# State space mixer: two x tiles projected as one seven-product pair in the first phase, parked in DRAM and read back

## The chip, the cores and the metric

The kernel runs on one core of a Trainium2 chip. The metric is the device time of one execution in microseconds (us); a kernel's time is the median of several executions.

## The reference

One layer of a hybrid sequence model over 1024 tokens with 1024 features, batch 1, all in float32. What matters here, cut down:

```python
u = rms_norm(h, norm_w)
proj = u @ w_in                                   # 1024 x 6668 outputs, then split:
q, f_logit, i_in, g_hg, u_pool, g_pool, xbc, dt_raw, z = jnp.split(proj, ...)
o_hg   = group_rms_norm(hgrn2_mixer(q, f_logit, i_in, lb), ...) * silu(g_hg)   # 6 heads
o_pool = pool_mixer(u_pool, ...) * silu(g_pool)                                # 4 groups
xbc    = silu(causal_conv4(xbc) + conv_b)         # 1792 channels = 14 tiles of 128
xs, bm, cm = split(xbc)                           # 6 x tiles, 4 B tiles, 4 C tiles
y_ssd  = ssd(xs, bm, cm, dt) * silu(z)            # state space mixer, 4 groups of 192 channels
h = h + concat(o_hg, o_pool, group_rms_norm(y_ssd, ...)) @ w_out
h = h + sigmoid(h @ w_pg) * (p @ w_pe)
return rms_norm(h, final_norm_w)
```

The change concerns x tiles 0 and 3 of `xbc`: how and when their 2 x 128 columns of `u @ w_in` are computed. State space group 0 needs x tiles 0 and 1, group 1 tiles 1 and 2, group 2 tiles 3 and 4, group 3 tiles 4 and 5.

## The kernel before

Every float32 product is made of three matmuls: each operand is split into a high part `hi` (ScalarE, line 168) and a remainder `lo` (VectorE, line 169), and `mm3` (lines 192 to 196) adds hi*hi, hi*lo and lo*hi in PSUM. The normalized and transposed input is kept split in SBUF as `uh`, `ul`.

Weights pass through a ring: SyncE (SP) loads a 512 KB piece into `raw` (two buffers, line 161), then it is split into `hi` and `lo` (four buffers each). So a piece can be split only when the piece four before it has been multiplied for the last time, and its load is issued when a `raw` buffer comes free.

A single channel tile is projected by `cm_proj` (lines 198 to 209): for each of two halves of the tokens 8 x 3 matmuls of 128x512 into one of two `pj` banks, then an evacuation. A pair of channel tiles can be projected by `st_cm` (lines 356 to 388) instead: seven products (Strassen's scheme in Winograd's form) of 4 x 3 matmuls, in the order 1, 5, 6, 2, 7, 3, 4, with seven evacuations (four copies on ScalarE, three additions on VectorE). The sums of `u` that it needs (`SH`, `SL`) lie in SBUF until `sst.close()`; the sums of weights are made in DRAM by GpSimd's DMA queue (`sums_by_dma`, lines 125 to 132): per pair eight copies and accumulating copies, of which six form a chain t3 = b22, t3 += b12, t2 = t3, t2 += b11, t4 = t2, t4 += b21. `st_cm_w(i)` (lines 346 to 354) loads and splits a pair's four weight pieces: w0 (products 1 and 2), w1 = t1, t3 (5 and 7), w2 = t2, t4 (6 and 4), w3 (3).

The phases: normalization and the V projections; four pairs for the pooling mixer by `st_cm` (lines 494 to 532, outputs in slots of an arena `bg`); two times three-way Z and G tiles by `st_tm` (lines 390 to 436); six heads of the gated recurrence (`hg_proj`, `hg_mix`, lines 563 to 728); then the state space phase (lines 733 to 860); gates, output projection and the end.

In the state space phase `plan` gives the order of tiles per group: B, C, then x. `conv_tile` (lines 733 to 751) projects a tile with `cm_proj`, evacuates each half twice on ScalarE (line 739 copies it to `xp`, line 740 writes scale * x + bias to `y`), adds the three shifted taps on VectorE (line 748) and applies Silu (line 749). `xp` and `y` are slots of a second arena, `ar`, which gives out the slot that has been free longest. `tok_x` transposes x tiles into `Y`. `ssd_group` (lines 763 to 822) runs eight chunks, and `y_fin` (lines 827 to 839) gates and normalizes, with gate tiles that take `ar` slots too.

A scheduler orders each engine's instructions by program order as priority, moved up for splits and evacuations, and by a simulated readiness; engines then run their queues in that order. So the projections of the next group's tiles fill TensorE between the small matmuls of `ssd_group`.

Of the kernel before, what the change touches and what calls it, by code (L numbers as in the profile page):

```python
# [9 lines left out]
F32 = mybir.dt.float32  # L10
# [7 lines left out]
P = 128  # L18
S = 1024
# [58 lines left out]
def body(ctx: ExitStack, tc: tile.TileContext, x, pT, wcm, wtm, wdt, wo, wg, we, nw, fw, cst, prm, out):  # L78
# [37 lines left out]

    PAIRS_C = ((26, 27), (30, 31), (28, 29), (32, 33))
    PAIRS_T = ((5, 6), (7, 2))
    tcd = [dp.tile([P, 2048], F32, name=f"tcd{i}") for i in range(4)]
    ttd = [dp.tile([P, 4096], F32, name=f"ttd{i}") for i in range(2)]  # L120
# [15 lines left out]
    def some_sums(ins, n):  # L136

        with tc.issue_after(ins.ins):
            for _ in range(n):
                if later:  # L140
                    later.pop(0)()
# [153 lines left out]
    xst.close()  # L295
    for d, (j0, j1) in zip(tcd, PAIRS_C):
        later += sums_by_dma([d[:, i * 512 : i * 512 + 512] for i in range(4)], wcm[j0][:, :512], wcm[j1][:, :512], wcm[j0][:, 512:], wcm[j1][:, 512:])
    for d, (s0, s1) in zip(ttd, PAIRS_T):
        later += sums_by_dma([d[:, i * 1024 : i * 1024 + 1024] for i in range(4)], wtm[2 * s0], wtm[2 * s1], wtm[2 * s0 + 1], wtm[2 * s1 + 1])
    some_sums(rooted, len(later))  # L300
    later += sums_by_dma([tod[i] for i in range(4)], *(wo[i, j] for i in range(2) for j in range(2)))
# [231 lines left out]


    gzd = dp.tile([P, NT, 1024], F32, name="gzd")
    for i in range(2):
# [184 lines left out]
    for h in range(HEADS):  # L721
        hg_proj(h)
        if h + 1 < HEADS:
            cm_want(2 * h + 2)
        else:
            cm_want(12)
        hg_mix(h)
# [5 lines left out]
    def conv_tile(j, nxt):  # L733
# [8 lines left out]
        cw = lambda i: pr[:, P_CW + 4 * j + i : P_CW + 4 * j + i + 1]  # L742
        cm_proj(12 + j, ev)
        if nxt is not None:
            cm_want(nxt)
        for i in range(3):
# [95 lines left out]
    plan = ((0, (6, 10, 0, 1)), (1, (7, 11, 2)), (2, (8, 12, 3, 4)), (3, (9, 13, 5)))  # L842
    order = [12 + j for _, js in plan for j in js]
    for g, js in plan:
        held = {}
        for j in js:
            i = order.index(12 + j)
            y, yh = conv_tile(j, order[i + 1] if i + 1 < len(order) else None)
            if j < 6:
                tok_x(j, y)  # L850
                ar.give(yh)
            else:
                held[j] = (y, yh)
# [372 lines left out]
```

## Time and profile before

| | |
|---|---|
| median of 3 runs | 1039.11 us (1036.5 to 1044.67) |
| profiled execution, its own time | 1037.42 us |
| its span in the trace | 1035.5 us |
| TensorE / weight loads / VectorE / ScalarE / GpSimd busy | 95% / 81% / 64% / 48% / 12% of the span |
| mean granted TensorE clock | 0.987 of full speed |

The working of the prediction is made against the profiled execution, 1037.42 us, because its durations come from there; 1.92 us of that lie outside the span. A busy share of TensorE counts overlapping matmuls once; the time that one matmul takes from the engine is read from the distance between the starts of successive ones. "Idle before" names the time an engine waited and the instruction that ended the wait.

### The profile page before, as it was taken

What the parts mean: (1) busy time and instruction counts of PE and PEld (TensorE: products, weight loads), DVE (VectorE), ACT (ScalarE), POOL (GpSimd) and SP (SyncE); (2) the same over time, 40 slices, a digit from 0 to 9 for tenths busy, and PEclk for the clock granted to TensorE, in tenths of its full rate; (3) what the DMA queues carried; (4) which work ended last, traced back from release to release, by engine and by line L of the source; (5) the groups of instructions that cost most, each with busy time, mean ns of one, the idle gap of its engine ahead of it and who ended that gap; (6) DMA issues with size and microseconds to landing.
All of it is one profiled execution on the core that took longest, in us unless ns stands there. A gap on an engine that the chain in (4) does not pass through costs nothing.

```text
span 1035.5 us, 17385 instructions
## 1 busy us (share of the span) xinstructions
PE 987.9 (95%) x6972; PEld 835.1 (81%) x6972; DVE 664.1 (64%) x1081; ACT 496.6 (48%) x924; POOL 128.1 (12%) x202
## 2 busy tenths in 40 slices
PE   8899999999999999998999999999969999999994
PEld 7899687999877877787878787799958888888883
DVE  5692547443286678667478885878246966565776
ACT  6442343544623332333557575778424333436765
POOL 2332210000001101110101010003323000000023
PEclk9989999999999999999999999999989999999997
DMA  7799982555715277451524543234499333224535
GB/s 297 191 193 244 245 214 89 180 165 153 236 42 178 65 167 203 130 168 37 121 87 117 142 123 95 81 92 165 157 338 418 104 113 100 83 82 165 165 117 204
DMA packets 62161, 162.28 MB, mean 157 GB/s; under 512 B 6368, under 2 KB 29248, under 8 KB 60352
## 3 DMA queue, kind: packets, MB, share of 16 engines
q1 hardware_dynamic: 45040, 91.88, 27.3%
q0 software_dynamic: 14592, 65.02, 23.7%
q10 hardware_dynamic: 2448, 4.26, 1.1%
q8 instruction: 55, 0.90, 0.4%
q14 instruction: 26, 0.21, 0.1%
HBM read 136.97 MB, written 66.11 MB: 196 GB/s over the span
## 4 chain that ended last, share of the span: by engine, by line
PE 74%; DVE 11%; DMA 4%; ACT 4%; issue 1%; POOL 1%; ACTq 0%; POOLq 0%; DVEq 0%; SPq 0%
PE b_pj L194 13%; PE b_pj L195 13%; PE b_pj L196 13%; PE b_mx L196 6%; PE b_mx L194 6%; PE b_mx L195 6%; DVE ar L582 5%; PE b_sc L194 2%; PE b_sc L195 2%; PE b_sc L196 2%; DVE lo L169 1%; ACT hi L168 1%; PE b_mx L806 1%; PE b_mx L871 1%; PE b_sc L704 1%
## 5 line engine op out<-in xcount | busy, mean ns | idle before, releaser
L169 DVE TENSOR_TENSOR lo<-raw,hi 128x1024 fp32r<-128x1024 f32 (+1 forms) x114 | 137.0, 1203 | 124.4 <-ACT hi L168 117.7
L168 ACT CAST hi<-raw 128x1024 fp32r<-128x1024 f32 (+1 forms) x114 | 117.7, 1035 | 132.9 <-PE b_pj L195 53.5
L194 PE MATMUL b_pj<-uh,hi 128*128 128x512 f32 x416 | 166.6, 400 | 2.1 <-ACT ar L740 1.7
L195 PE MATMUL b_pj<-ul,hi 128*128 128x512 f32 x416 | 167.7, 403 | 0.0
L196 PE MATMUL b_pj<-uh,lo 128*128 128x512 f32 x416 | 167.2, 402 | 0.0
L194 PE MATMUL b_pj<-hi,uh 128*128 128x256 f32 (+1 forms) x320 | 93.5, 292 | 4.9 <-ACT vs L258 4.6
L582 DVE TENSOR_TENSOR ar<-ar 128x512 f32<-128x512 f32 (+8 forms) x168 | 93.9, 594 | 6.4 <-PE b_sc L673 4.9
L194 PEld LDWEIGHTS b_pj<-uh,hi 128*128 128x128 f32 x416 | 78.3, 188 | 18.8 <-ACT ar L740 3.1
L195 PE MATMUL b_pj<-lo,uh 128*128 128x256 f32 (+1 forms) x320 | 92.1, 288 | 0.0
L196 PE MATMUL b_pj<-hi,ul 128*128 128x256 f32 (+1 forms) x320 | 91.8, 287 | 0.2 <-DVE ul L247 0.2
L195 PEld LDWEIGHTS b_pj<-ul,hi 128*128 128x128 f32 x416 | 78.3, 188 | 16.9
L196 PEld LDWEIGHTS b_pj<-uh,lo 128*128 128x128 f32 x416 | 78.2, 188 | 15.8
L194 PE MATMUL b_mx<-hi,ah 128*128 128x512 f32 x192 | 76.6, 399 | 5.1 <-ACT ah L983 5.1
L983 ACT CAST ah<-q 128x1024 fp32r<-128x1024 f32 x36 | 37.5, 1048 | 84.9 <-PE b_mx L195 47.0
L196 PE MATMUL b_mx<-hi,al 128*128 128x512 f32 x192 | 75.9, 395 | 0.4 <-DVE al L984 0.4
L195 PE MATMUL b_mx<-lo,ah 128*128 128x512 f32 x192 | 76.2, 397 | 0.0
L984 DVE TENSOR_TENSOR al<-q,ah 128x1024 fp32r<-128x1024 f32 x36 | 43.7, 1222 | 47.2 <-ACT ah L983 47.2
L194 PEld LDWEIGHTS b_pj<-hi,uh 128*128 128x128 f32 x320 | 61.6, 193 | 5.6 <-ACT vs L258 4.8
L195 PEld LDWEIGHTS b_pj<-lo,uh 128*128 128x128 f32 x320 | 61.5, 192 | 0.7 <-DVE lo L169 0.5
L196 PEld LDWEIGHTS b_pj<-hi,ul 128*128 128x128 f32 x320 | 61.4, 192 | 0.5 <-DVE ul L247 0.4
L748 DVE SCALAR_TENSOR_TENSOR ar<-ar,pr 128x1021 f32<-128x1021 f32 (+2 forms) x42 | 53.7, 1279 | 2.8 <-ACT ar L740 2.3
L194 PEld LDWEIGHTS b_mx<-hi,ah 128*128 128x128 f32 x192 | 36.4, 190 | 13.9 <-ACT ah L983 5.5
(296 smaller groups left out, 2130.8 us busy)
## 6 DMA issues: line engine op xcount, KB each, us to landing
raw<-wcm SPq DMA_DIRECT2D x30, 512.0 KB, 4.4
tod<-wo POOLq DMA_DIRECT2D x4, 2048.0 KB, 15.2
raw<-tod SPq DMA_DIRECT2D x16, 512.0 KB, 3.3
raw<-wtm SPq DMA_DIRECT2D x14, 512.0 KB, 4.2
tcd<-wcm POOLq DMA_DIRECT2D x24, 256.0 KB, 8.0
ttd<-wtm POOLq DMA_DIRECT2D x12, 512.0 KB, 8.6
E<-cumd SPq DMA_DIRECT2D x32, 192.0 KB, 3.1
mt<-ar POOLq DMA_DIRECT2D x24, 256.0 KB, 2.5
```

Source lines behind the costliest of these rows:

```text
L168: A.copy(hi[:, :width], raw[:, :width])
L169: V.tensor_tensor(out=lo[:, :width], in0=raw[:, :width], in1=hi[:, :width].bitcast(F32), op=ALU.subtract)
L194: T.matmul(out=o, lhsT=sh, rhs=mh, start=first, stop=False, skip_group_check=more)
L195: T.matmul(out=o, lhsT=sh, rhs=ml, start=False, stop=False, skip_group_check=more)
L196: T.matmul(out=o, lhsT=sl, rhs=mh, start=False, stop=last, skip_group_check=more)
L582: mul = lambda o, x, y: V.tensor_tensor(out=o, in0=x, in1=y, op=ALU.mult)
L704: T.matmul(out=sb[:, :P], lhsT=kt3[:, c, :], rhs=O[:, c, hv], start=True, stop=True)
L748: V.scalar_tensor_tensor(out=y[:, d:], in0=xp[:, : S - d], scalar=cw(i), in1=y[:, d:], op0=ALU.mult, op1=ALU.add)
L806: T.matmul(out=b2[r, i * 64 : i * 64 + 64], lhsT=E[:, i, r], rhs=xd[:, c % 4, i * 64 : i * 64 + 64], start=True, stop=True)
L871: T.transpose(out=b[:, i * P : (i + 1) * P], in_=src[:, half * 4 + i, k * P : (k + 1) * P], identity=ident)
L983: A.copy(hi, src)
L984: V.tensor_tensor(out=lo, in0=src, in1=hi.bitcast(F32), op=ALU.subtract)
```

## The change

A fifth pair, wcm tiles 12 and 15 (x tiles 0 and 3), is added to the pairs. Its weight sums are issued on GpSimd's queue behind those of the `ttd` pairs. After the pooling loop and ahead of `st_tm` it is projected with `st_cm` into two slots of `bg`, and each slot is stored to a DRAM tile `park`. In the state space phase `conv_tile` loads `xp` for these tiles from DRAM on SP's queue and writes `y` with one ScalarE instruction over 1024 tokens, where it projected them and evacuated the halves. The prefetch of weights follows: the two tiles leave the list `order`, and behind the last head the first piece asked for is that of tile 18 (B of group 0), where it was tile 12.

```diff
--- before.py
+++ after.py
@@ -114,9 +114,11 @@
     ones = cs[:, C_ONE : C_ONE + P]
 
 
-    PAIRS_C = ((26, 27), (30, 31), (28, 29), (32, 33))
+    PAIRS_C = ((26, 27), (30, 31), (28, 29), (32, 33), (12, 15))
+    PARKED = [j for p in PAIRS_C[4:] for j in p]
+    parkd = {j: dp.tile([P, S], F32, name=f"park{j}") for j in PARKED}
     PAIRS_T = ((5, 6), (7, 2))
-    tcd = [dp.tile([P, 2048], F32, name=f"tcd{i}") for i in range(4)]
+    tcd = [dp.tile([P, 2048], F32, name=f"tcd{i}") for i in range(5)]
     ttd = [dp.tile([P, 4096], F32, name=f"ttd{i}") for i in range(2)]
 
     tod = dp.tile([4, 4 * P, 1024], F32, name="tod")
@@ -293,10 +295,12 @@
     nc.sync.dma_start(cs, cst[:, P:])
     nc.sync.dma_start(pr, prm)
     xst.close()
-    for d, (j0, j1) in zip(tcd, PAIRS_C):
+    for d, (j0, j1) in zip(tcd[:4], PAIRS_C):
         later += sums_by_dma([d[:, i * 512 : i * 512 + 512] for i in range(4)], wcm[j0][:, :512], wcm[j1][:, :512], wcm[j0][:, 512:], wcm[j1][:, 512:])
     for d, (s0, s1) in zip(ttd, PAIRS_T):
         later += sums_by_dma([d[:, i * 1024 : i * 1024 + 1024] for i in range(4)], wtm[2 * s0], wtm[2 * s1], wtm[2 * s0 + 1], wtm[2 * s1 + 1])
+    for d, (j0, j1) in zip(tcd[4:], PAIRS_C[4:]):
+        later += sums_by_dma([d[:, i * 512 : i * 512 + 512] for i in range(4)], wcm[j0][:, :512], wcm[j1][:, :512], wcm[j0][:, 512:], wcm[j1][:, 512:])
     some_sums(rooted, len(later))
     later += sums_by_dma([tod[i] for i in range(4)], *(wo[i, j] for i in range(2) for j in range(2)))
     later += sums_by_dma([tgd[i] for i in range(4)], *(wg[i, j] for i in range(2) for j in range(2)))
@@ -530,6 +534,14 @@
             bg.give(Uh)
         bg.give(G0h)
         bg.give(G1h)
+
+
+    W = st_cm_w(4)
+    outs = [bg.take(1024) for _ in range(2)]
+    st_cm(W, outs[0][0], outs[1][0])
+    for j, (z, zh) in zip(PAIRS_C[4], outs):
+        nc.sync.dma_start(parkd[j], z)
+        bg.give(zh)
 
 
     gzd = dp.tile([P, NT, 1024], F32, name="gzd")
@@ -723,7 +735,7 @@
         if h + 1 < HEADS:
             cm_want(2 * h + 2)
         else:
-            cm_want(12)
+            cm_want(12 + 6)
         hg_mix(h)
 
 
@@ -740,9 +752,13 @@
             A.activation(y[:, c], b, AF.Identity, scale=cw(3), bias=pr[:, P_CB + j : P_CB + j + 1])
 
         cw = lambda i: pr[:, P_CW + 4 * j + i : P_CW + 4 * j + i + 1]
-        cm_proj(12 + j, ev)
-        if nxt is not None:
-            cm_want(nxt)
+        if 12 + j in PARKED:
+            nc.sync.dma_start(xp, parkd[12 + j])
+            A.activation(y, xp, AF.Identity, scale=cw(3), bias=pr[:, P_CB + j : P_CB + j + 1])
+        else:
+            cm_proj(12 + j, ev)
+            if nxt is not None:
+                cm_want(nxt)
         for i in range(3):
             d = 3 - i
             V.scalar_tensor_tensor(out=y[:, d:], in0=xp[:, : S - d], scalar=cw(i), in1=y[:, d:], op0=ALU.mult, op1=ALU.add)
@@ -840,11 +856,11 @@
 
 
     plan = ((0, (6, 10, 0, 1)), (1, (7, 11, 2)), (2, (8, 12, 3, 4)), (3, (9, 13, 5)))
-    order = [12 + j for _, js in plan for j in js]
+    order = [12 + j for _, js in plan for j in js if 12 + j not in PARKED]
     for g, js in plan:
         held = {}
         for j in js:
-            i = order.index(12 + j)
+            i = order.index(12 + j) if 12 + j in order else len(order)
             y, yh = conv_tile(j, order[i + 1] if i + 1 < len(order) else None)
             if j < 6:
                 tok_x(j, y)
```

## Rows read from the trace of the kernel before

**Rows 1.** The page, part 1: busy time, share of span, instructions

```profile
PE 987.9 (95%) x6972; PEld 835.1 (81%) x6972; DVE 664.1 (64%) x1081; ACT 496.6 (48%) x924; POOL 128.1 (12%) x202
```

**Rows 2.** The page, part 4: chain that ended last, by engine

```profile
PE 74%; DVE 11%; DMA 4%; ACT 4%; issue 1%; POOL 1%; ACTq 0%; POOLq 0%; DVEq 0%; SPq 0%
```

**Rows 3.** Busy time per stretch: stretch, length, engines, clock, DMA share, GB/s

```profile
95.00:185.00 90.00, 87.36 (x364) 66.39 (x363) 51.61 (x83) 34.65 (x51) 11.19 (x16) 1.00 0.74 195
130.00:160.00 30.00, 30.00 (x131) 24.21 (x130) 14.62 (x16) 11.65 (x15) 2.80 (x5) 1.00 0.86 221
160.00:185.00 25.00, 23.79 (x97) 17.43 (x96) 17.28 (x26) 10.68 (x15) 0.00 (x0) 1.00 0.25 83
...
496.20:528.40 32.20, 32.20 (x151) 26.59 (x152) 16.17 (x16) 15.78 (x30) 4.70 (x4) 1.00 0.52 124
528.40:577.00 48.60, 46.99 (x302) 38.25 (x301) 39.21 (x73) 32.23 (x73) 4.62 (x6) 1.00 0.44 125
577.00:637.30 60.30, 59.54 (x365) 48.67 (x364) 44.17 (x78) 38.63 (x83) 4.62 (x6) 1.00 0.40 114
637.30:687.00 49.70, 48.61 (x336) 40.20 (x335) 40.86 (x78) 35.59 (x77) 2.58 (x4) 1.00 0.30 88
```

**Rows 4.** TensorE's instructions in order of time (start, duration): a pair's product; the Z and G tiles' first

```profile
95.12 0.40 PE L194 MATMUL b_pj<-sh,hi 128*128 128x512 f32 x1
...
97.91 0.39 PE L194 MATMUL b_sc<-uh,hi 128*128 128x512 f32 x1
...
184.70 0.28 PE L194 MATMUL b_mx<-hi,uh 128*128 128x256 f32 x1
```

**Rows 5.** The same, one half of x tile 0's projection: 24 matmuls

```profile
501.77 0.39 PE L194 MATMUL b_pj<-uh,hi 128*128 128x512 f32 x1
...
507.21 0.40 PE L194 MATMUL b_pj<-uh,hi 128*128 128x512 f32 x1
```

**Rows 6.** ScalarE in order of time, the hand-over behind the fourth pair

```profile
177.78 1.05 ACT L168 CAST hi<-raw 128x1024 fp32r<-128x1024 f32 x1 [2.05 <-PE b_sc L195]
```

**Rows 7.** GpSimd's queue in order of time, the tail of the weight sums

```profile
113.19 0.84 POOL L129 DMA_DIRECT2D tcd<-wcm  x1 [1.26 <-DMA tcd<-tcd]
...
129.29 0.81 POOL L129 DMA_DIRECT2D ttd<-wtm  x1 [5.77 <-DMA ttd<-ttd]
...
152.64 0.81 POOL L129 DMA_DIRECT2D ttd<-wtm  x1 [6.88 <-DMA ttd<-ttd]
```

**Rows 8.** DMA issues: count, KB each, median us to landing

```profile
raw<-wcm SPq DMA_DIRECT2D x30, 512.0 KB, 4.4
...
tcd<-wcm POOLq DMA_DIRECT2D x24, 256.0 KB, 8.0
...
raw<-tcd SPq DMA_DIRECT2D x8, 512.0 KB, 6.9
```

**Rows 9.** Groups of ScalarE's instructions, 496 to 710 us: busy, mean ns, idle before

```profile
L740 ACT ACTIVATE ar<-b_pj,pr 128x512 f32<-128x512 f32 x26 | 20.2, 779 | 0.0
...
L749 ACT ACTIVATE ar<-ar 128x1024 f32<-128x1024 f32 x13 | 13.8, 1059 | 16.5 <-DVE ar L748 16.5
L168 ACT CAST hi<-raw 128x1024 fp32r<-128x1024 f32 x13 | 13.6, 1044 | 11.9 <-PE b_pj L195 11.9
```

**Rows 10.** VectorE in order of time, between state space groups 1 and 2

```profile
605.86 0.95 DVE L833 TENSOR_TENSOR ar<-ar 128x768 f32<-128x768 f32 x1
...
607.92 1.22 DVE L169 TENSOR_TENSOR lo<-raw,hi 128x1024 fp32r<-128x1024 f32 x1
609.06 3.92 DVE L748 SCALAR_TENSOR_TENSOR ar<-ar,pr 128x1021 f32<-128x1021 f32 x3
...
617.62 3.92 DVE L748 SCALAR_TENSOR_TENSOR ar<-ar,pr 128x1021 f32<-128x1021 f32 x3
```

**Rows 11.** VectorE in order of time, within the last head's mixing

```profile
471.77 0.35 DVE L884 SCALAR_TENSOR_TENSOR big<-big,rsh,ar 128x128 f32<-128x128 f32 x1 [1.86 <-DMA ar<-gzd]
```

**Rows 12.** Waits of TensorE, 458 to 493 us: total, times, longest

```profile
PE b_sc L595 <- DVE ar L582: 3.2, 2, 2.7
```

## The prediction, written before the change was run

> **What bounds the kernel now.** I read the page's shares of busy time first [rows 1]: TensorE is busy for 95% of the span and its weight loads for 81%, VectorE for 64%. The chain that ended last says the same in its own way: 74% of it lies on TensorE, 11% on VectorE [rows 2]. A busy TensorE is not yet a bound, so I went to the stretches that the change touches [rows 3]. From 95 to 185 us, where the pairs of the pooling mixer run, TensorE is busy for 87.4 of 90 us; in the four stretches of the state space phase it stands still for 0.0, 1.6, 0.8 and 1.1 us. In both places a matmul taken away or added is therefore time, to first order. The second reading of the same rows is VectorE: 51.6 of 90 us in the first phase, but 39.2 of 48.6, 44.2 of 60.3 and 40.9 of 49.7 us around groups 1 to 3. There it is the engine that is next to bind once TensorE has less to do.
>
> **The matmuls.** The distance between the starts of two products of a pair is 97.91 - 95.12 = 2.79 us for twelve matmuls, 0.2325 us each [rows 4]. A half of x tile 0's projection takes 507.21 - 501.77 = 5.44 us for 24 matmuls, 0.2267 us each [rows 5]. The change removes two tiles of 2 x 24, which is 96 matmuls or 21.8 us, from the state space phase, and adds seven products of twelve, which is 84 matmuls or 19.5 us, to the first phase. The balance is -2.3 us: this is all that the arithmetic can give, 0.2% of the time. Whatever waits arise at either end are of the same size, so the rest of the working is about those.
>
> **First phase, the new pair itself.** It starts where the Z and G tiles start now, at 184.70 us [rows 4]. Its four pieces are split as the fourth pair lets go of its own. In the present hand-over to the Z tiles the same thing is seen: the first split of the next weights starts at 177.78 us, released by a product of the pair still running [rows 6], seven us ahead of the first use. So the hand-over costs nothing as long as the pieces are there; without that cover it would be a load and a split, 4.4 + 1.0 + 1.2 us [rows 8, 9, 10]. The added splits and evacuations (3.5 pieces on both engines, four evacuations on ScalarE and three on VectorE, each at most as long as a split; so at most 8 us on either by [rows 9, 10]) lie in a phase where VectorE is idle for 38 of 90 us and ScalarE for 55 [rows 3]. They cost nothing. The two stores to DRAM wait on SP for the last evacuation; the loads of the next weights run ahead of them in the ring, as the pooling outputs' stores do now. I put them at nothing, and at one load, 4.4 us [rows 8], if they stand ahead of a weight load.
>
> **The weight sums.** Eight more DMAs on GpSimd's queue, six of them in a chain, are behind the `ttd` pairs. The queue waits for each link: its last issue now is at 152.64 us, one pair's last addition comes 16 us (113.19 to 129.29) or 23 us (129.29 to 152.64) behind the previous one's [rows 7]. By that distance the new pair's last addition is issued at 169 to 176 us and lands some 8 us later [rows 8], at 177 to 184. It is needed by product 6, two products into the pair, at 184.7 + 5.6 = 190.3 us, less a split of 1 to 2 us and a load of 4.4 to 6.9 [rows 8]: the sums have to have landed by 181 to 184. This just fits. From below: behind 152.64 nothing else uses the queue and the DMA share falls from 0.86 to 0.25 [rows 3], so links would be faster and the cost is nothing. From above: if the whole chain began only at 152.64, six links of 8 us end at 200 us, 17 us late. Pairs are interleaved on this queue, or their last additions could not lie 16 and 23 us apart where six links of 8 us make 48; so I take the lower end, zero.
>
> [...]
>
> The other price of the sums is that they share the DMA engines with weight loads. `raw<-tcd` loads, which run beside the sums, take 6.9 us where the weight loads as a whole take 4.4 [rows 8]. I add 1 us for the fourth pair's later loads, between 0 and 2.5 us (that difference).
>
> **State space phase, x tile 0.** Around group 0 VectorE is busy for 16.2 of 32.2 us [rows 3]. With 10.9 us of matmuls gone it has 14.9 us of work left in 21.3 (one split of 1.22 less [rows 10]), ScalarE about 13.6. The chain that follows the last projected tile (evacuation, taps, Silu, transposes) is still covered by the next group's matmuls. Its load waits for a slot that head 5 frees at its end, and the taps fall where VectorE had gaps. I put it at 0.5 us, between 0 and 2.
>
> **State space phase, x tile 3.** This one is tighter. The stretch from 577.0 to 637.3 us would become 49.4 us with 42.9 us of VectorE work. Its neighbours, with three projected tiles each, are the best row for what such a stretch needs: VectorE is idle there for 48.6 - 39.2 = 9.4 and 49.7 - 40.9 = 8.8 us [rows 3]. If this stretch needs 9.1 as well, it lasts 52.0 us, and 2.6 us of the gain go back. The mechanism that I expect is a slot. The `xp` of tile 3 lies where `y_fin` of group 1 has its gate tiles, whose last use starts at 605.86 us [rows 10]; then load (4.4), ScalarE (1.1) and the taps (3.9) bring tile 3 to about 616. `y` of tile 4 gets the slot of tile 3's `xp`, so its evacuation (L740) can't be written before that, though its first half is projected by about 611. ScalarE and then a `pj` bank wait behind it. From below 0, if VectorE fills its gaps; from above 8 us, when the tile's whole taps, load and write-out become exposed (3.9 + 4.4). I take 2.6.
>
> ScalarE itself is relieved: at least four L740 evacuations and two splits (5.2 us) against two passes of 1.06 us [rows 9].
>
> **The changed prefetch.** Tile 18 is asked for before the last head's mixing, not behind it. Its matmuls run within that mixing today, so its weights are there in time, and I count nothing. VectorE waits there 1.86 us for a DMA of a gate that was moved up [rows 11], and TensorE once 2.7 us for VectorE [rows 12]; that wait may move or go, 0 to -2.7.
>
> **Sum.** 1037.4 - 21.8 + 19.5 + 1 (loads beside the sums) + 0.5 (tile 0) + 2.6 (tile 3) = 1039.2 us. This is against the profiled execution; the median of the runs shown is 1.7 us above it, so 1039 is also the median of before. A measurement of this kernel can tell about 1% (10 us) from no change.
>
> **Rivals.**
> *The sums are late* (slower). Place: SP's load of t2, t4, behind which stand w3 and the Z pieces. It decides from a landing at 184 us; each us after that is a us. Against it: the fill of earlier gaps. For it: the distance of 23 us, by which it lands at 184, and the extra traffic. Time 1039 + 5 = 1044, at the far end 1039 + 17 = 1056.
> *VectorE and the slots take tile 3's gain* (slower). If tile 4's evacuation stands in ScalarE's queue ahead of what VectorE needs, the 8 us are exposed: 1039.2 - 2.6 + 8 = 1045; with 2 us at tile 0, 1047. For it: 87% of VectorE in that stretch. Against it: the stretches at 81 and 82% run with TensorE idle for 1.6 and 1.1 us.
> *All of the gain is kept* (faster). VectorE's idle 16 us around group 2 shrink with the stretch, no wait arises, and the 2.7 us wait in the last head goes: 1037.4 - 2.3 - 2.7 = 1032.4.
>
> **Chances.** Forecast (1035 to 1043) 0.58; late sums 0.16; VectorE and slots 0.14; all kept 0.12. The range reaches to the faster rival and over the near part of both slower ones, 1032 to 1049. Slower by over 1% of 1039.1 (above 1049.5) needs the far half of the late sums, or both slower rivals together: 0.11. Faster by over 1% (below 1028.7) would need more waits to go than the rows show: 0.04. Within 1%: 0.85.
>
> **What would show it.** The tiles of the new pair: 84 matmuls in 19.5 us, no idle time of TensorE before its third product (else the sums are late, with SP's wait on `tcd` beside it). The last `tcd` addition on GpSimd's queue at 169 to 176 us. The stretch around group 0 at 21 to 22 us and around group 2 at 50 to 53. Idle time of TensorE ended by L740 in the latter would be the slot. It would be wrong if the phases between, the heads or the end, change their own length: nothing that I found moves work into them but two memsets of `big` that shift behind the Z tiles, into idle time of VectorE.

## The result, and the profile after

The changed kernel takes 1051.0 us (1049.1 to 1053.7) against 1039.2 for the kernel before beside it: a ratio of 1.0107, 95% interval 1.0083 to 1.0131. It is 1.1% slower, outside the range of 1032 to 1049. The profiled execution of after has 1050.76 us of its own and a span of 1048.9; that of before has 1037.42 and 1035.5.

The page of after, part 1 and the first line of part 4 (compare [rows 1, 2]):

```profile
PE 991.7 (95%) x6960; PEld 836.0 (80%) x6960; DVE 667.5 (64%) x1086; ACT 494.9 (47%) x922; POOL 131.7 (13%) x210
PE 68%; DVE 13%; DMA 6%; ACT 5%; issue 1%; POOL 1%; POOLq 0%; ACTq 0%; DVEq 0%; SPq 0%
```

The shares of busy time hardly move, and there are twelve matmuls fewer, yet TensorE is busy for 3.8 us more. In the chain TensorE's part falls from 74% to 68% and that of DMAs rises from 4% to 6%. VectorE's part rises from 11% to 13%. The page says that waits came in, not where. For that I laid landmarks of TensorE's timeline side by side: the distance from the start of one landmark to the next, in one profiled execution of each kernel.

```
stretch (us)                            before    after   forecast  after - before
start to the small matmuls (bcum)       102.26    97.91   as before      -4.35
bcum to the end of the fourth pair       82.44    92.15   +1             +9.71
the new pair                               -      19.45   19.5          +19.45
Z products, to head 0's first scores    107.37   107.96   as before      +0.59
heads 0, 1, 2 (three stretches)         103.90   104.13   as before      +0.23
heads 3 and 4                            69.32    72.38   as before      +3.06
head 5 to group 0, group 0 to 1         112.90   102.31   -10.4         -10.59
group 1 to 2, group 2 to 3              109.04   105.77   -8.3           -3.27
group 3 to the fills, and the rest      348.27   346.84   as before      -1.43
```

The matmuls came out as worked: the new pair takes 19.45 us, and what x tile 0 gives is within 0.2 us. Four lines are off by several microseconds: the start, the four old pairs, heads 3 and 4, and x tile 3. The start's -4.35 us is idle time of TensorE: 9.3 us before, 4.9 after; its longest wait there, for a ScalarE evacuation of the V projections, lasts 4.6 us before and 2.2 after. None of the added instructions runs in that stretch, and over the runs below its length moves by as much.

**The old pairs.** Waits of TensorE in after between 97 and 191 us (total, times, longest); in order of time three splits of ScalarE and one of VectorE with what they waited for; last, before's split that stands for the one at 139.30:

```profile
PE b_mx L196 <- ACT big L373: 5.2, 4, 3.0
PE b_sc L522 <- DVE big L516: 3.7, 1, 3.7
...
139.30 1.05 ACT L170 CAST hi<-raw 128x1024 fp32r<-128x1024 f32 x1 [7.36 <-DMA raw<-tcd]
158.51 1.05 ACT L170 CAST hi<-raw 128x1024 fp32r<-128x1024 f32 x1 [3.84 <-DMA raw<-tcd]
164.28 0.62 ACT L170 CAST hi<-raw 128x512 fp32r<-128x512 f32 x1 [4.72 <-DMA raw<-wcm]
164.93 0.69 DVE L171 TENSOR_TENSOR lo<-raw,hi 128x512 fp32r<-128x512 f32 x1 [4.05 <-ACT hi L170]
...
140.18 1.05 ACT L168 CAST hi<-raw 128x1024 fp32r<-128x1024 f32 x1 [4.13 <-DMA raw<-tcd]
```

While ScalarE waits 7.36 us for the sums of a later pair, the evacuation of a finished product (L373) stands behind that split in its order of time, at 142.62 us, and TensorE waits for that product's bank, 3.02 us up to 145.20. The load that it waits for takes 8.8 us from issue to landing, 5.6 in before, where the split waits 4.13 us and TensorE does not wait behind it. The wait of 3.7 us goes through VectorE's queue: the split at 164.93 stands still for 4.05 us, and behind it stand the pooling additions (165.54 to 172.84 us) whose result L522 multiplies. In before TensorE waits 2.6 us in this stretch, in after 9.1. Most of the rest of the 9.71 us is the clock (stretch, length, busy time of the five engines, granted clock, DMA share, GB/s):

```profile
97.90:190.06 92.16, 83.20 (x330) 62.02 (x331) 44.99 (x63) 32.40 (x46) 15.85 (x23) 0.96 0.79 197
144.00:152.00 8.00, 6.80 (x29) 5.56 (x30) 2.64 (x5) 3.29 (x5) 1.09 (x2) 1.00 1.02 335
172.00:180.00 8.00, 7.10 (x13) 3.61 (x13) 3.64 (x8) 1.87 (x3) 0.00 (x0) 0.61 0.14 25
172.90:180.00 7.10, 7.10 (x13) 3.61 (x13) 2.74 (x6) 1.87 (x3) 0.00 (x0) 0.63 0.03 6
190.06:209.52 19.46, 19.46 (x86) 15.75 (x85) 9.15 (x10) 7.25 (x10) 0.00 (x0) 1.00 0.50 170
```

Behind the idle time of 3.71 us (it ends at 172.90) the granted clock is 0.63 for 7.1 us, 0.50 up to 178.0 and 0.95 in the last 2 us; if TensorE's time goes with the clock, that is 7.1 x 0.37 = 2.6 us, an estimate. At 0.50 one matmul of 512 columns follows another after 0.42 us there (176.91 and 177.33), against 0.23 us at 1.00 [rows 4]. Behind the 3.02 us at 145.20 it stays at 1.00. The last row is the new pair: no idle time in it at all.

**x tile 3.** After, in order of time, the engines around group 2:

```profile
623.41 0.95 DVE L849 TENSOR_TENSOR ar<-ar 128x768 f32<-128x768 f32 x1
624.38 0.32 SPq L756 DMA_DIRECT2D ar<-park  x1
631.85 1.23 ACT L757 ACTIVATE ar<-ar,pr 128x1024 f32<-128x1024 f32 x1
633.11 1.28 DVE L764 SCALAR_TENSOR_TENSOR ar<-ar,pr 128x1021 f32<-128x1021 f32 x1 [0.76 <-ACT ar L757]
635.60 0.96 DVE L855 TENSOR_TENSOR ar<-ar,rsy 128x768 f32<-128x768 f32 x1 [1.21 <-POOL rsy L158]
636.48 2.60 DVE L764 SCALAR_TENSOR_TENSOR ar<-ar,pr 128x1022 f32<-128x1022 f32 x2
639.17 1.45 ACT L752 ACTIVATE ar<-b_pj,pr 128x512 f32<-128x512 f32 x2 [2.90 <-DVE ar L764]
640.00 0.80 PE L196 MATMUL b_pj<-uh,hi 128*128 128x512 f32 x1 [4.38 <-ACT ar L752]
```

This is the chain of the prediction, link for link: the gate's multiplication frees the slot (623.41), the parked tile's load is issued, ScalarE's pass, the taps, then tile 4's evacuation (L752), which has stood still for 2.90 us, and TensorE, which has stood still for 4.38. Only the length differs: from the gate to the end of the taps it takes 639.08 - 623.41 = 15.7 us where the prediction had 10. ScalarE first evacuates a half of tile 12, loads a table (1.28 us) and applies Silu to tile 8 (the pass starts 7.5 us behind the load's issue, not 4.4), and `y_fin`'s last product (L855), itself waiting for GpSimd, stands between the first and the second tap. The clock then does the rest, on the same columns:

```profile
640.00:645.00 5.00, 5.00 (x15) 4.12 (x16) 4.96 (x8) 1.89 (x3) 0.00 (x0) 0.50 0.84 211
645.00:652.20 7.20, 7.13 (x41) 5.85 (x40) 1.41 (x3) 4.07 (x8) 0.00 (x0) 0.94 0.37 109
```

Five microseconds at 0.50 and 7.2 at 0.94 cost 2.5 + 0.4 = 2.9 us, by the same estimate; from 640.59 to 643.15 us one matmul of 512 columns follows another after 0.43 us. With the 4.38 that is 7.3, of the 10.9 - 3.3 = 7.6 us that tile 3 lost.

**Heads 3 and 4.** Both have a wait of TensorE that before does not have. After, TensorE in order of time, and the stretch between the two:

```profile
435.30 0.21 PE L607 MATMUL b_sc<-ar 128*32 128x16 f32 x2 [1.22 <-issue]
471.60 0.26 PE L607 MATMUL b_sc<-ar 128*32 128x16 f32 x8 [1.55 <-issue]
...
435.30:471.60 36.30, 33.65 (x383) 27.28 (x382) 24.61 (x55) 12.23 (x32) 3.34 (x4) 1.00 0.59 154
```

"issue" means that the profile shows nothing that was waited for. Both stand inside a run of 64 small score products, ahead of the last 2 and the last 8. From the one to the other there are 383 matmuls and 382 weight loads. Nothing in the change touches the heads; what it does is to put 84 matmuls, with as many weight loads, ahead of them in TensorE's stream. That became a theory of its own.

The page's list of DMA queues has one more row that bears on it, `q8 instruction`; here it is for the whole of after, and for 432.9 to 433.0 and 469.3 to 469.4 us (transfers that start there, MB, share of the DMA engines):

```profile
q8 instruction: 54, 0.88, 0.3%
...
q8 instruction: 1, 0.02, 55.9%
...
q8 instruction: 1, 0.02, 58.9%
```

Each of the 54 transfers is 16,384 bytes, and there is one for every 258 of the 13,920 matmuls and weight loads: by that count I take it that TensorE's own instructions come in; the trace does not show what a transfer holds. One starts 2.4 us before the first wait ends, one 2.2 us before the second.

### The profile page after: what moved, and what is told of

Read it like the earlier page. It is cut to its first block, busy times and chain, and to the rows that moved or that the text cites. A ratio compares the mean times of both kernels' runs of the same rounds, so it can differ in the third digit from the quotient of the medians.

```text
span 1048.9 us, 17396 instructions
## 1 busy us (share of the span) xinstructions
PE 991.7 (95%) x6960; PEld 836.0 (80%) x6960; DVE 667.5 (64%) x1086; ACT 494.9 (47%) x922; POOL 131.7 (13%) x210
## 4 chain that ended last, share of the span: by engine, by line
PE 68%; DVE 13%; DMA 6%; ACT 5%; issue 1%; POOL 1%; POOLq 0%; ACTq 0%; DVEq 0%; SPq 0%
PE b_pj L196 11%; PE b_pj L197 11%; PE b_pj L198 10%; PE b_mx L196 6%; PE b_mx L198 6%; PE b_mx L197 6%; DVE ar L594 5%; PE b_sc L196 2%; PE b_sc L197 2%; PE b_sc L198 2%; DMA raw<-tcd 2%; DMA E<-cumd 2%; ACT hi L170 2%; DVE lo L171 2%; PE b_mx L822 1%
## 5 line engine op out<-in xcount | busy, mean ns | idle before, releaser
L170 ACT CAST hi<-raw 128x1024 fp32r<-128x1024 f32 (+1 forms) x116 | 119.5, 1032 | 135.7 <-PE b_pj L197 46.8
L196 PE MATMUL b_pj<-uh,hi 128*128 128x512 f32 x384 | 154.9, 404 | 6.1 <-ACT ar L752 6.1
L198 PE MATMUL b_pj<-uh,lo 128*128 128x512 f32 x384 | 155.8, 406 | 0.0
L197 PE MATMUL b_pj<-ul,hi 128*128 128x512 f32 x384 | 155.8, 406 | 0.0
L196 PEld LDWEIGHTS b_pj<-uh,hi 128*128 128x128 f32 x384 | 72.8, 190 | 21.6 <-ACT ar L752 6.9
L197 PEld LDWEIGHTS b_pj<-ul,hi 128*128 128x128 f32 x384 | 72.7, 189 | 16.0
L198 PEld LDWEIGHTS b_pj<-uh,lo 128*128 128x128 f32 x384 | 72.7, 189 | 14.7
L1000 DVE TENSOR_TENSOR al<-q,ah 128x1024 fp32r<-128x1024 f32 x36 | 43.7, 1223 | 50.2 <-ACT ah L999 50.2
```

Of the source, the lines that this page charges most:

```text
L170: A.copy(hi[:, :width], raw[:, :width])
L196: T.matmul(out=o, lhsT=sh, rhs=mh, start=first, stop=False, skip_group_check=more)
L197: T.matmul(out=o, lhsT=sh, rhs=ml, start=False, stop=False, skip_group_check=more)
L198: T.matmul(out=o, lhsT=sl, rhs=mh, start=False, stop=last, skip_group_check=more)
L1000: V.tensor_tensor(out=lo, in0=src, in1=hi.bitcast(F32), op=ALU.subtract)
```

## The experiments

Three theories, each with its rivals. *Traffic*: the eight sums take DMA time that weight loads need. *Slot*: tile 3's place in the third group makes tile 4 wait. *Position*: the heads wait for instructions at places that the 84 added matmuls have shifted. All ratios are against runs of the kernel before on the same chip.

### The sums alone, added to the kernel before

```diff
+    for d, (j0, j1) in zip(tcd[4:], ((12, 15),)):
+        later += sums_by_dma([d[:, i * 512 : i * 512 + 512] for i in range(4)], wcm[j0][:, :512], wcm[j1][:, :512], wcm[j0][:, 512:], wcm[j1][:, 512:])
```

The lines stand behind those of the `ttd` pairs; no instruction reads these sums.

> The kernel before with nothing added but the eight DMAs that make the weight sums of a fifth pair, which nobody reads. Theory A (the sums cost by standing in the way of the weight loads): the pooling pairs end 5 us later than at 184.7 us, with waits of ScalarE for raw<-tcd and raw<-wcm and of TensorE for an evacuation behind them, and the time is 1039.1 + 5.4 = 1044.5 us (1043 to 1046). Theory B (the waits that the changed kernel shows there come with its run, whose first 95 us were 4.4 us shorter, and are not caused by the sums): no change, 1039 us (1037.5 to 1040.5).

Measured: 1045.8 us, ratio 1.0053 (1.0024 to 1.0083), so 5.5 us (2.5 to 8.6). Old pairs 92.88 us, heads 3 and 4 at 34.6 and 34.7, the way from head 5 to group 0 1.7 us longer, the other groups as before. TensorE's waits between 98 and 192 us, and ScalarE's split that stands for the 7.36 us of after:

```profile
PE b_mx L194 <- ACT big L371: 5.1, 2, 3.5
PE b_sc L520 <- DVE big L514: 2.8, 1, 2.8
PE b_sc L520 <- DVE big L515: 1.4, 1, 1.4
...
142.14 1.05 ACT L168 CAST hi<-raw 128x1024 fp32r<-128x1024 f32 x1 [7.86 <-DMA raw<-tcd]
```

It follows that the sums alone bring the stall of the old pairs, without a new matmul.

### The new pair with plain weights, without the sums

```diff
-    for d, (j0, j1) in zip(tcd[4:], PAIRS_C[4:]):
-        later += sums_by_dma([d[:, i * 512 : i * 512 + 512] for i in range(4)], wcm[j0][:, :512], wcm[j1][:, :512], wcm[j0][:, 512:], wcm[j1][:, 512:])
-        w1 = wsplit(wload(tcd[i][:, :1024], 1024), 1024)
+        w1 = wsplit(wload(tcd[i][:, :1024] if i < 4 else wcm[j0], 1024), 1024)
-        w2 = wsplit(wload(tcd[i][:, 1024:], 1024), 1024)
+        w2 = wsplit(wload(tcd[i][:, 1024:] if i < 4 else wcm[j1], 1024), 1024)
```

> The changed kernel without the eight DMAs of the fifth pair's sums: its pieces w1 and w2 are loaded from the weights themselves, so x tiles 0 and 3 are not the reference's and the output is another. Everything else is as in the changed kernel. Theory A: the waits of the pooling pairs go and 5.4 us come back, 1045.6 us (1044 to 1047). Theory B: 1051 us (1049.5 to 1052.5).

Measured: 1048.7 us, ratio 1.0083 (1.0058 to 1.0108). Old pairs 82.25 us; the same split of ScalarE waits 2.97 us. Heads 3 and 4 at 35.7 and 36.2, group 0 to 1, 1 to 2 and 2 to 3 at 50.2, 54.4 and 50.8. The stretch agrees with the traffic. In the time, though, taking the sums out of the changed kernel gives 2.5 us where adding them to the kernel before cost 5.5; the intervals overlap. One reason is that the moment at which the old pairs begin varies between executions as well (97.9 to 104.5 us over these kernels, the shifted starts below aside), and a late begin meets fewer of the sums. Over all profiles, the stretch is 87.5 to 92.9 us in the six with early sums and 81.8 to 86.8 in the eight without; they begin 1.9 us earlier with the sums, by the means, and end 5.2 later. The begin counts by itself: of the eight, the three that begin at 99.1 to 100.0 us need 84.9 to 85.8, the four that begin behind 102.2 need 81.8 to 82.4 (the eighth, the removal in the new order, begins at 102.12 and needs 86.79); among the six the begin makes no such order. By the eight, some 3 us of after's 9.71 may go with its early begin, so the table's first two lines are best read together. The load behind the split takes 7.6 to 9.3 us in the six and 4.4 to 8.9 in the eight: it is not the sums alone that slow it. I put the sums at 2.5 to 5.5 us.

### A slot of its own for the parked tile

```diff
+    xpk = a2p.tile([P, 1024], F32, name="xpk")
-        (xp, xh), (y, yh) = ar.take(1024), ar.take(1024)
+        (xp, xh) = (xpk, None) if 12 + j in PARKED else ar.take(1024)
+        y, yh = ar.take(1024)
```

> The changed kernel, with a tile of its own for what is read back from DRAM, so that neither that load nor the output of tile 4 waits for a slot in turn. Slot theory: the stretch between the first TensorE product of group 1 and of group 2, now 55.9 us, falls to 49 to 51 us, the 4.4 us of idle time of TensorE and the stretch at the lower clock behind it go, and the time is 1051 - 6 = 1045 us (1043.5 to 1046.5). Rival (VectorE is short of time there, whatever the slots): the stretch stays at 54 to 56 us and the time at 1050 us (1049 to 1052).

Measured: 1049.2 us, ratio 1.0093 (1.0057 to 1.0128). Group 1 to 2, then 2 to 3: 48.5 and 50.3 us (after: 55.9 and 49.9), and the longest wait of TensorE there is 1.3 us. The slot was the cause. The time barely moves, because the way to head 0 is 5.6 us longer (113.55 us): with a free slot the parked tile's load is issued early, ahead of others on SP, ScalarE waits 7.3 us for a load of E and TensorE 3.0 us for ScalarE's evacuation. The repair made a new wait on a queue:

```profile
282.69 0.41 SPq L759 DMA_DIRECT2D xpk<-park  x1
308.05 1.28 ACT L802 ACTIVATE E<-E,sm 128x128 f32<-128x128 f32 x4 [7.27 <-DMA E<-cumd]
313.31 0.79 PE L196 MATMUL b_pj<-uh,hi 128*128 128x512 f32 x1 [3.04 <-ACT ar L586]
```

### The third group takes tile 3 first

```diff
-    plan = ((0, (6, 10, 0, 1)), (1, (7, 11, 2)), (2, (8, 12, 3, 4)), (3, (9, 13, 5)))
+    plan = ((0, (6, 10, 0, 1)), (1, (7, 11, 2)), (2, (3, 8, 12, 4)), (3, (9, 13, 5)))
```

> The changed kernel with one line different: the third group takes x tile 3 from DRAM before it projects tiles 8 and 12, instead of behind them. Slot theory: the tile's load no longer waits for the gate tiles of the group before, and no evacuation waits for its taps. Group 1 to group 2 (first products with E of each) takes 49 to 51 us instead of 55.9, the longest idle time of TensorE there stays under 1.5 us and the granted clock stays at 0.9 or more; the kernel takes about 1046 us. Rival (VectorE has too much work in that stretch, wherever the tile stands): 54 to 56 us, no gain, about 1051 us. Neither theory moves the heads or the first phase.

Measured: 1044.4 us, ratio 1.0031 (1.0007 to 1.0055): 6.6 us below the changed kernel by the medians, which come from two chips, and 7.9 by the ratios. Group 1 to 2: 52.1 us, a microsecond more than expected; groups 0 to 3 together 201.6 us against 208.1. Order of time, and the only longer wait of TensorE there:

```profile
610.72 1.24 ACT L757 ACTIVATE ar<-ar,pr 128x1024 f32<-128x1024 f32 x1 [0.28 <-PE b_sc L818]
613.96 0.95 DVE L849 TENSOR_TENSOR ar<-ar 128x768 f32<-128x768 f32 x1
...
PE b_pj L196 <- ACT ar L752: 1.6, 2, 1.2
```

The parked tile's pass now stands ahead of the gate's multiplication, not 8 us behind it. The rival, too much work for VectorE, falls. Of the 21.8 us that the removed matmuls are worth, the groups now keep 221.9 - 201.6 = 20.3.

### Position: tiny matmuls in the kernel before, and in the changed one

```diff
+    tiny = bank("sc")
+    for i in range(84):
+        T.matmul(out=tiny[:, :16], lhsT=uh[:, 0, :P], rhs=uh[:, 0, :16], start=True, stop=True)
```

These lines stand ahead of the Z products. The changed kernel gets the same with 44 in place of 84.

> The kernel before with 84 matmuls of 16 columns added ahead of the Z products (their result is not used): as many TensorE instructions as the new pair has, with next to no work, no weights, no transfers. Theory that the heads' new idle times come from the position of the instructions in TensorE's stream: the two idle times without a releaser ahead of score products appear in heads 3 and 4, 1 to 1.8 us each, and these two heads last 1.3 to 1.8 us longer than the 34.6 us of before. Rival (something that the pair leaves behind, such as its stores or a shifted order of the loads): heads 3 and 4 stay at 34.6 us. The time itself: before + 5 to 8 us for the 84 matmuls, and + 3 us by the theory.

Measured: 1056.5 us, ratio 1.0161 (1.0130 to 1.0192). Heads 3 and 4 take 36.6 and 36.0 us, and the two waits are there, ahead of the last 2 and the last 8 again:

```profile
426.68 0.21 PE L600 MATMUL b_sc<-ar 128*32 128x16 f32 x2 [1.83 <-issue]
...
462.48 0.26 PE L600 MATMUL b_sc<-ar 128*32 128x16 f32 x8 [1.02 <-issue]
```

The price of the 84 was missed: they take 12.9 us (185.30 to 198.23), and the Z products behind them 2.7 us more. The first part of that row of matmuls and the rest, on the columns of [rows 3]:

```profile
185.30:190.80 5.50, 5.50 (x51) 5.50 (x49) 4.90 (x5) 2.79 (x4) 0.00 (x0) 0.98 0.75 233
190.90:198.20 7.30, 7.30 (x36) 7.30 (x36) 0.89 (x1) 0.00 (x0) 0.00 (x0) 0.50 0.35 134
```

TensorE never stands still in it, and yet the granted clock falls to 0.50; one of these matmuls follows another after 0.11 us at first and after 0.21 then.

> The changed kernel with 44 matmuls of 16 columns added ahead of the Z products (their result is not used). If what counts in the heads is where the instructions lie in TensorE's stream, a further shift moves the idle times elsewhere in a head, and may put them where TensorE is not short of instructions: heads 3 and 4 then last 34.6 us instead of 36.0 and 36.4, at a price of 2.5 to 4 us for the 44 matmuls. Rival (the position plays no part): both heads stay at 36.0 and 36.4 us, with the waits ahead of the same products.

Measured: 1059.5 us, ratio 1.0188 (1.0173 to 1.0203). Heads 3 and 4 take 34.62 and 34.75 us, no such wait is left anywhere in the heads; the stretch from head 3 to head 5 falls from 72.4 to 69.4 us. The 44 cost 6.6 us, again more than expected, and the Z products behind them take 1.4 us more. So 84 added matmuls bring the waits and 128 take them away, whatever the matmuls compute: the position theory stands.

From the first wait to the second there are 382 matmuls and 382 weight loads (the row above counts one at its border), in each of the seven kernels that have the waits: 764 instructions. Before has 55 transfers of 16,384 bytes on the queue `q8 instruction` for 13,944 matmuls and weight loads, one for every 253.5, and after 54 for 13,920, one for every 257.8; over all kernels there are 54 or 55 for 13,752 to 14,112. So 764 instructions are about three transfers, and in after the one ahead of the second wait (469.36 us) is the third behind the one ahead of the first (432.93). By the same counts, an estimate, 128 added matmuls with their loads, 256 instructions, are about one transfer: they would put the transfers back to where none added leaves them.

That TensorE waits for such a transfer is inferred from when the waits end. There are 14 of them, 0.9 to 1.8 us long, and whatever its length each ends 2.2 to 2.5 us after a transfer has started (in after 2.37 and 2.24). In the seven kernels without the waits no transfer starts from 6.7 us ahead of that run of 64 products to 3.1 us behind its start, in either head (in before's head 4 the nearest start 7.8 us ahead and 3.8 us behind). The added matmuls move the transfers, and the waits come and go with them. No run slows a transfer by itself. Why this run of products shows the wait is an argument: its 64 products of 16 columns take 0.74 us together in before, less than the 2.2 us, where 24 matmuls of 512 columns take 5.44 [rows 5].

### The removal alone, in the old order and in the new

```diff
-    for d, (j0, j1) in zip(tcd[4:], PAIRS_C[4:]):
-        later += sums_by_dma([d[:, i * 512 : i * 512 + 512] for i in range(4)], wcm[j0][:, :512], wcm[j1][:, :512], wcm[j0][:, 512:], wcm[j1][:, 512:])
...
-    W = st_cm_w(4)
-    outs = [bg.take(1024) for _ in range(2)]
-    st_cm(W, outs[0][0], outs[1][0])
...
-            nc.sync.dma_start(xp, parkd[12 + j])
+            nc.sync.dma_start(xp, wcm[12 + j])
```

> The change without the new pair and without its eight weight sums: x tiles 0 and 3 are read from DRAM where another array of that size stands (their values are not the reference's), so only the removal of the 96 matmuls is left. By the working of the prediction, with tile 3's slot at the 6.5 us that the changed kernel shows: 1037.4 - 21.8 + 0 + 6.5 = about 1022 us, group 0 in 52 us, group 1 to 2 in 55 to 56 us, heads at 34.6 us each and the stretch of the pooling pairs at 82 us. Rival (the tail of the kernel gives part of it back, or the heads' waits come from reading the parked tiles): 1027 us or more, or heads 3 and 4 at 36 us.

Measured: 1028.4 us, ratio 0.9890 (0.9860 to 0.9920). Heads at 34.6 to 34.7 us, group 0 to 1 and 1 to 2 at 49.7 and 54.2, old pairs 82.2. The groups keep 221.9 - 206.5 = 15.4 of the 21.8 us and so lose 6.4, as expected. But by the medians only 12 us are gained, and the time is where the rival has it; in the profiled execution the remaining 3 us lie ahead of the pairs (104.47 us) and in the last stretch (326.7), where executions differ by as much.

> The removal of the 96 matmuls alone (x tiles 0 and 3 read from another array in DRAM, so their values are not the reference's; no pair, no sums), with x tile 3 taken first in the third group. If the slot was all that was lost of the removal, groups 0 to 3 take 201 to 203 us together (222 in the kernel before, 206 in the removal with the old order) and the kernel about 1024 us, 4 us below the removal with the old order. If VectorE's load is what keeps part of it back, they stay at 206 us and the kernel at 1028 us.

Measured: 1023.5 us, ratio 0.9842 (0.9811 to 0.9873), as expected; groups 0 to 3 together 201.6 us. So the new order is worth 4.9 us here and 6.6 in the changed kernel, and the removal at its best is worth 16 us. A pair that takes 19.45 us can't be paid from that. This profile also shows that the old pairs are near a stall even without the sums (on the columns of [rows 3], and a wait):

```profile
140.00:150.00 10.00, 6.83 (x30) 5.20 (x29) 4.28 (x4) 6.31 (x8) 0.81 (x1) 0.99 0.57 132
150.00:160.00 10.00, 10.00 (x39) 7.96 (x38) 3.30 (x5) 2.70 (x3) 1.35 (x2) 0.84 0.70 238
...
PE b_mx L196 <- ACT big L371: 3.3, 2, 3.2
```

The stretch took 86.79 us there, the longest without sums.

### The pair behind the Z products, and the causes mended together

```diff
-    W = st_cm_w(4)
...
     for i in range(2):
...
         st_tm(i, gz_fin)
+    W = st_cm_w(4)
...
+            if g == 2:
+                with tc.issue_after(G.tensor_copy(out=seen0, in_=U[:, 0:1]).ins):
+                    while fifth:
+                        fifth.pop(0)()
```

The pair moves as a whole; its sums, in `fifth`, are issued behind the third pooling tile. In the second kernel below they are issued behind the fourth (`g == 3`), and the third group has the new order as well.

> The changed kernel with the fifth pair behind the Z and G tiles, and its sums issued only when the pooling mixer's third group has its first output, past the loads that they slowed. Theory A: the pooling pairs end at 181 to 185 us without the waits on raw<-tcd, the pair costs its 19.5 us elsewhere, and 1051 - 5.4 = 1045.6 us result (1044 to 1047.5). Theory B: 1050 to 1052 us, since nothing that matters was moved.

Measured: 1049.0 us, ratio 1.0080 (1.0048 to 1.0112). Old pairs 84.9 us, the Z products at 184.84 us (184.70 in before), Z products and pair 127.3 us, where 107.37 + 19.45 = 126.8 are expected from the two apart. Heads 3 and 4 at 36.6 and 37.0, group 0 to 1 and 1 to 2 at 52.5 and 54.7, the rest at 327.0. The traffic is gone from the old pairs; heads and groups keep their loss.

> Two of the causes mended together: the new pair stands behind the Z products and its weight sums are issued behind the last pooling tile, and the third group takes x tile 3 first. If the causes are apart and add up, the first phase up to the Z products takes 82.5 to 85 us, the Z products and the new pair together 127 us, groups 0 to 3 together 202 to 204 us (222 in the kernel before), heads 3 and 4 still 36.5 and 37 us, and the kernel about 1044 us. Rival (the causes share a resource and do not add up): over 1048 us.

Measured: 1044.1 us, ratio 1.0046 (1.0028 to 1.0064), as expected in time. Old pairs 85.8, Z products and pair 129.2 (2 more than expected), heads 3 and 4 at 36.2 both, groups together 200.7 us. But the new order alone already took 1044.4: moving pair and sums adds nothing to it. The old pairs end 4.2 us earlier; 1.8 are lost in the Z products and the pair, 2.0 in the stretch behind the state space groups (326.7 against 324.7 us). In the kernels with the early pair that last stretch took 323.4 to 325.1 us, in the others 325.6 to 327.0. Why is open; TensorE's idle time behind group 3 is much the same in both (7.8 to 8.8 us).

The last two runs move the heads' instructions from the very start of the kernel instead:

```diff
-    for i in range(WARM):
-        T.matmul(out=warm[:, :256], lhsT=blk[0].rearrange("p c t -> p (c t)")[:, :P], rhs=blk[1].rearrange("p c t -> p (c t)"), start=True, stop=True)
+    for i in range(WARM + 22):
+        n = 256 if i < 4 else 32
+        T.matmul(out=warm[:, :n], lhsT=blk[0].rearrange("p c t -> p (c t)")[:, :P], rhs=blk[1].rearrange("p c t -> p (c t)")[:, :n], start=True, stop=True)
```

`WARM` is 7; this is an edit of the changed kernel. Each of these f32 matmuls leaves two matmul records in the trace (14 for the 7 of before, 58 for the 29 here), so by the records 22 more move the stream by 44 places.

> The changed kernel with the same 22 further small matmuls among the warm-up matmuls at the very start and nothing else. Position theory: heads 3 and 4 last 34.6 us instead of 36.0 and 36.4, so about 1048 us, 3 us less than the changed kernel. Rival (the added matmuls ahead of the Z products had changed something else in the heads): heads as in the changed kernel, 1051 us.

Measured: 1056.4 us, ratio 1.0165 (1.0135 to 1.0194). The heads did what the position theory says: 34.61 and 34.80 us, no such wait. The time rose nevertheless, and the start says why (the shifted kernel first, then before: the warm-up matmuls, the first transposes behind them, and a stretch on the columns of [rows 3]):

```profile
1.38 11.19 PE L154 MATMUL b_sc<-blk,blk 128*128 128x256 f32 x58 [1.38 <-POOL blk L150]
12.38 1.95 PE L241 MATMUL b_mx<-ident,x 128*128 128x128 f32 x8
...
10.00:20.00 10.00, 9.30 (x43) 8.56 (x42) 4.12 (x6) 4.76 (x8) 2.37 (x4) 0.50 0.84 345
```

```profile
1.38 5.50 PE L151 MATMUL b_sc<-blk,blk 128*128 128x256 f32 x14 [1.38 <-POOL blk L148]
8.48 1.09 PE L238 MATMUL b_mx<-ident,x 128*128 128x128 f32 x8 [1.61 <-DVE x L229]
...
10.00:20.00 10.00, 8.51 (x62) 7.33 (x62) 8.61 (x11) 7.78 (x15) 3.62 (x8) 1.00 0.97 398
```

The added matmuls don't fit into the time in which TensorE waits: the warm-up lasts until 12.57 us, and the first transposes start at 12.38 (8.48 in before, 8.12 in after). And the granted clock is 0.50 from 10 to 20 us, where before has 1.00 and after 0.83. The bcum landmark comes at 104.94 us, not at after's 97.91. My "no cost" was wrong. The edit adds narrow matmuls and narrows three wide ones; which of the two the clock follows is not shown.

The same edit in the kernel with the late pair and the new order:

> The kernel with the late pair and the new order, with 22 further small matmuls among the warm-up matmuls at the very start (three of the wide ones become narrow), where TensorE waits for its first input. This moves every later TensorE instruction by as many places as the 44 small matmuls of the other run did, at no cost. Position theory: heads 3 and 4 last 34.6 us again, 4 us less than without the shift, and the kernel takes about 1040 us, the time of before: the change can then be had for nothing, but gains nothing either. If this beats before by more than 3 us, the working of what the pair itself costs is too high; if the heads keep 36.5 and 37 us, the shift's place matters and not its size.

Measured: 1049.6 us, ratio 1.0088 (1.0053 to 1.0122). Heads 3 and 4 at 34.6 and 34.9, 2.8 us less than without the shift; the start costs 8.6 us more (107.69). Had the shift been free, 1044.1 - 2.8 would be about 1041 us: no version of this change that these runs point to is faster than the kernel before.

## Why the prediction was wrong

**Arithmetic.** Right for the matmuls. 84 matmuls in 19.45 us, no idle time in the pair; the sums' last `tcd` addition on GpSimd's queue lies at 169.48 us, within 169 to 176:

```profile
153.81 0.83 POOL L131 DMA_DIRECT2D ttd<-wtm  x1 [5.91 <-DMA ttd<-ttd]
...
169.48 0.80 POOL L131 DMA_DIRECT2D tcd<-wcm  x1 [4.05 <-DMA tcd<-tcd]
```

The rival of the late sums is out. The hand-over to the pair, the stores, and the changed prefetch cost nothing that can be seen; tile 0 lost 10.9 - 10.59 = 0.3 us, the forecast was 0.5. One comparison is off: the sum of 1039.2 is built on a profiled execution of 1037.4 and so says 1.8 us more than before, but it was set beside before's median, as no change. Like for like it is 1040.9 by the medians.

**The loads beside the sums: the term was mis-sized, 1 us forecast, 5.5 measured alone (2.5 to 8.6).** The step that failed is "I add 1 us for the fourth pair's later loads, between 0 and 2.5 us (that difference)". It priced the traffic as a longer latency of one load. But the engines were full there: the share of 0.86 stood in [rows 3] and was read as a background. From 100 to 170 us, stretch by stretch of 10 us, the DMA shares add up to 5.80 in before and 6.60 in after: 8 us more of full occupation, and 2 MB at the 221 GB/s of [rows 3] would have said 9.5. Weight loads that were due beside it came late (8.8 us for the one that ScalarE waited for, 9.3 in the kernel with the sums alone, 5.6 in before, though up to 8.9 in one kernel without sums), the queues of ScalarE and VectorE carried the delay to TensorE, and the clock added to it. The sum of the prediction should have held this as a time of a full resource.

**Tile 3: the mechanism was right, the term was mis-sized, 2.6 us forecast, 7.6 measured.** The failing step is to take 2.6 from the neighbours' idle time of VectorE, while the slot's chain, named two sentences on, gives the later date. Two of its links were too short, and a stall of 4.4 us was priced as 4.4 us: the granted clock of 0.50 and 0.94 behind it adds 2.9 by the estimate above. The bound of 8 us held. The rival on VectorE and the slots named place and chain, but priced 1045 to 1047 by itself, since it was the only slower term at work in it.

**The heads: 3.1 us forecast as nothing.** The prediction says that it would be wrong if the heads changed their own length, and they did, by a cause that no row of before shows: with the 84 added matmuls TensorE has two waits without a releaser, of 1.22 and 1.55 us, that end 2.4 and 2.2 us after a transfer on the instruction queue starts. That it waits there for its own instructions is inferred from these times and from the counts. The shift by 84 matmuls is enough to bring it and a further 44 to remove it.

**Sum.** 11.6 us lie between the sum of 1039.2 and the profiled execution of after, 1050.76. Start and old pairs together 9.7 - 4.35 - 1 = 4.4 (the sums measured alone would give 5.5 - 1 = 4.5), tile 3 7.6 - 2.6 = 5.0, heads 0 to 4 3.3, Z products 0.6, tile 0 -0.2, the rest -1.4: 11.7. The traffic's part is the least sure (2.5 us by the other pair of kernels); the Z products and the rest are not explained, nor why the start differs between executions.

**The chances.** 0.11 on slower by over 1% needed "the far half of the late sums, or both slower rivals together"; it came from the second rival, a term with too narrow bounds and a cause unseen. Three small terms, each allowed to err only on its own, were added as if a stall cost its length.

## What to carry to other kernels

Where the DMA engines are full, price an added transfer by its bytes at the rate of that stretch (here 9.5 us of DMA time by that rate, 8 by the shares, of which 2.5 to 5.5 us reached the kernel's time), and follow which load it puts off and which engine's queue passes the delay on (here ScalarE's, which waited 7.36 us, and VectorE's, 4.05). Price an expected stall of TensorE of 4 us at some 1.7 times its length if the profile shows the clock falling behind such stalls (here, by the clock, 4.38 us cost 2.9 more, 3.71 us 2.6 more, and 3.02 us nothing; but behind the 3.04 us of the run with a slot of its own one matmul of 512 columns followed another after 0.43 us for 5 us), and follow a slot to its date link by link rather than by an engine's idle share. A change of TensorE's instruction count can bring waits into code that it doesn't touch (here 3.1 us in heads 3 and 4): compare stretch by stretch, look for "issue", and for a transfer on the instruction queue just ahead of it (here 2.2 to 2.5 us before the wait ends).

## What the runs showed that I had not expected

In heads 3 and 4 TensorE has waits of 0.9 to 1.8 us without a releaser whose place follows the count of instructions ahead of them: absent with 0 and with 128 added matmuls, present with 84: four kernels with 0, three with 128, seven with 84, and each of them fits. Each of the 14 waits ends 2.2 to 2.5 us after a transfer of 16,384 bytes on the instruction queue starts. A matmul of 16 columns costs 0.11 us in a row of such at a granted clock of 0.98 and 0.21 at 0.50, against 0.23 us at 1.00 of one with 512 columns [rows 4], and in a row of 84 without a pause the clock fell to 0.50. And 22 added warm-up matmuls, with three narrowed, held the first transposes back by 4 us and left the clock at 0.50 from 10 to 20 us, at a cost of 7 to 9 us.
